# A hybrid attention and SSD layer on one core: output weights split early and loaded in the last attention pair, a four-step combine, and an output projection in a hand-written order

## The chip, the cores and the metric

One core of a Trainium2 chip. The metric is the device time of one execution in microseconds (us), as the median over runs. Engine names are those of the profile: PE (matrix multiplies), DVE, ACT and POOL (elementwise work), SP (issues most of the DMAs). POOL issues DMAs on a queue of its own.

## The reference

One decoder layer on x of shape (1, 2048, 1024), all in float32. An input projection gives q, k, v, the two gates z and the input of the SSD mixer. Attention runs three times per head (16 heads of 64) with dilations 1, 4 and 16 and a window of 128 steps; the three results are weighted by a softmax over their log-sum-exps. The SSD mixer is a chunked scan over 16 chunks of 128. Both branches are gated and normalised and meet in the output projection:

```python
y_att = (wts[0][..., None] * o1 + wts[1][..., None] * o2 + wts[2][..., None] * o3)
y_att = rms_norm(y_att.reshape(Bsz, S, D_ATT) * jax.nn.silu(z_att), att_norm_g[layer])
...
y_ssm = rms_norm(y.reshape(Bsz, S, D_SSM) * jax.nn.silu(z_ssm), ssm_norm_g[layer])
mix = jnp.concatenate([y_att, y_ssm], axis=-1)
out = jnp.einsum('bsd,de->bse', mix, w_out[layer])
x = layer_norm(alpha * x + out, ln_g[layer], ln_b[layer])
```

## The kernel before

Every large product is made of three matmuls on numbers split in two: a rounded high part (hi) and the remainder (lo), as hi·hi + hi·lo + lo·hi.

**Stages.** Projections of v, the gates and the convolution inputs come first, one `proj` per 128 output columns, 96 matmuls of 128x512 each. Then the eight projections of the SSD gate (`proj(32 + i)`, to about 685 us). From 685 to 1268 us q, k and the remaining gates are projected, with the 32 SSD units `ssd(n, g)` (chunk n, half g of the heads) between them; a unit stores its gated result y in `d_us`. Attention follows from 1268 us, in 8 pairs of heads, and then the output projection, to 2213 us.

**A pair of heads.** The loop `todo` runs over pairs, three dilations d, four blocks qd and two halves: 24 steps a pair. A step makes scores (L503), exponentials on ACT (L519), two steps later transposes (L532, copied to PT by DVE, L534) and one step after that the values (L552). After the last step of d=1 and of d=2 `statistics` transposes the minima and sums and SP stores them in `d_st` in short runs; `gather` reads them back as `cm` (L586). In the next pair DVE and ACT make the softmax weights from cm (`weights`, L593 to L603), SP stores them in `d_wd` and loads them broadcast over 64 partitions into `wb` (L616), and POOL combines the three results of the pair before (`combine`: L618, L627), gates them (L632), and SP stores the result in `d_ua`. Only pair 7 is combined by DVE, into four PT tiles. POOL also permutes q for d=1 (L467) and d=2 (L471) and issues the loads of k and q of the next pair (`load_qk`, L437), 1 MB each.

**The order.** Inside `tc.manual_schedule` PE, DVE, ACT and POOL take their instructions in the order in which the code is written; SP's order there, and all orders elsewhere, are set by the scheduler. An engine's queue is in order: an instruction that waits holds up all that stand behind it. Tiles of one name share a ring of buffers (three `v`, six `num`, three `wb`, four `qp`, three `P`), so a load waits until the tile that it replaces has been read.

**The output projection**, outside the manual order, multiplies 16 rows of 128 tokens by 2048x1024 weights: 32 products `product(n, br)` (row n; br=1 the SSD half, 0 the attention half) of 48 matmuls (L716 to L718). Weights are loaded raw, multiplied by the norm's gain and split on ACT, DVE or POOL (`prep_w`, L650 to L655) just ahead of use. `load_u` loads a row, splits it (L684, L685), sums its squares (L686, L688), and PE multiplies the sums by a column of ones (L690). `norm` is the layer norm.

## Time and profile before

| | |
|---|---|
| median of 3 runs | 2223.53 us (2221.91 to 2236.11) |
| profiled execution: its own time | 2223.12 us |
| profiled execution: span | 2221.3 us, mean granted PE clock 0.977 |
| instructions | 36859 |
| PE busy | 2152.9 us (97% of the span) |
| DVE, ACT, POOL busy | 1130.6, 867.1, 756.7 us |
| DMA | 321.69 MB, mean 145 GB/s |
| PE idle before L552 (values), ended by a PT copy of DVE | 27.7 us, 8 times |
| PE idle before L716 (product), ended by ACT's split of a weight (qp) | 12.2 us, once |

A row of the busy times reads: microseconds, share of the span, number of instructions. A row of a stretch gives its bounds and length, then busy time and instructions of PE, of PE's weight loads, of DVE, ACT and POOL, then the granted PE clock (1 is full), the share of the 16 DMA engines and GB/s. A row of the waits gives the waiting instruction, what ended the wait, the microseconds in all, the number of times and the longest. A row of the chain of waits or of the timeline begins with start and duration.

### The profile page before, as it was taken

The numbers are of one execution on the slowest core, as the hardware profiler recorded it, in microseconds if no ns is written. First come the engines' busy times: TensorE is split into PE (matmuls) and PEld (weight loads), VectorE is DVE, ScalarE is ACT, GpSimd is POOL, SyncE is SP. The second block draws the span as 40 slices with busy tenths as digits, with TensorE's granted clock in tenths as the row PEclk, the third lists the DMA queues.
The fourth block names the chain that finished last, engine by engine and source line by source line (L and its number), as shares of the span: only waits on it lengthen the run. The fifth ranks groups of instructions, "written<-read, shape, count | busy, mean of one in ns | idle before, by whom it ended". The sixth has DMA issues, their size and how long they took to land.

```text
span 2221.3 us, 36859 instructions
## 1 busy us (share of the span) xinstructions
PE 2152.9 (97%) x13968; PEld 1794.0 (81%) x13968; DVE 1130.6 (51%) x2931; ACT 867.1 (39%) x2318; POOL 756.7 (34%) x511
## 2 busy tenths in 40 slices
PE   8999999999999999999999999999989987999998
PEld 8999888888888888888888788778777865888886
DVE  4000265643003555454544278778777886655553
ACT  4101122223112233322355378778777864322221
POOL 3101010101112465555555313466544682221211
PEclk9999999999999999999999989999999987999999
DMA  8544222223125455555543536767677556422220
GB/s 284 176 134 135 82 68 76 67 76 91 58 85 178 174 190 174 177 182 175 189 140 126 199 122 189 225 186 201 185 209 213 153 168 184 135 97 95 82 83 29
DMA packets 239361, 321.69 MB, mean 145 GB/s; under 512 B 36304, under 2 KB 173648, under 8 KB 230992
## 3 DMA queue, kind: packets, MB, share of 16 engines
q1 hardware_dynamic: 234576, 285.78, 42.4%
q0 software_dynamic: 4608, 33.56, 4.0%
q8 instruction: 110, 1.80, 0.3%
q14 instruction: 67, 0.55, 0.1%
HBM read 205.65 MB, written 113.64 MB: 144 GB/s over the span
## 4 chain that ended last, share of the span: by engine, by line
PE 86%; DMA 7%; issue 2%; DVE 2%; POOL 1%; ACT 1%; SPq 1%; DVEq 0%; ACTq 0%; POOLq 0%
PE pp L111 14%; PE pp L109 14%; PE pp L110 14%; PE S L503 6%; PE N L552 6%; PE T L532 5%; PE S L716 4%; PE S L717 4%; PE S L718 3%; PE pp L153 2%; PE pp L154 2%; PE pp L152 2%; DMA d_st<-sT 2%; PE T L716 2%; PE T L717 2%
## 5 line engine op out<-in xcount | busy, mean ns | idle before, releaser
L109 PE MATMUL pp<-xh,whi 128*128 128x512 f32 x1408 | 550.2, 391 | 0.0
L110 PE MATMUL pp<-xl,whi 128*128 128x512 f32 x1408 | 549.5, 390 | 0.0
L111 PE MATMUL pp<-xh,wlo 128*128 128x512 f32 x1408 | 548.7, 390 | 0.0
L519 ACT ACTIVATE P<-P,st 128x256 f32<-128x256 f32 (+1 forms) x768 | 345.1, 451 | 94.5 <-DVE st L511 93.8
L111 PEld LDWEIGHTS pp<-xh,wlo 128*128 128x128 f32 x1408 | 264.3, 188 | 55.2
L109 PEld LDWEIGHTS pp<-xh,whi 128*128 128x128 f32 x1408 | 264.4, 188 | 54.7
L110 PEld LDWEIGHTS pp<-xl,whi 128*128 128x128 f32 x1408 | 264.4, 188 | 54.2
L511 DVE CUSTOM_DVE_ANT_0 P<-S,tb 128x256 f32<-128x256 f32 (+1 forms) x768 | 235.2, 362 | 105.7 <-PE S L503 51.2
L99 POOL TENSOR_TENSOR wlo<-wraw,whi 128x1024 fp32r<-128x1024 f32 x44 | 106.1, 2412 | 489.8 <-ACT whi L98 489.8
L552 PE MATMUL N<-PT,v 128*64 128x128 f32 x2400 | 183.3, 291 | 27.7 <-DVE PT L534 27.7
L534 DVE COPY PT<-T 128x512 f32<-128x512 f32 (+1 forms) x304 | 196.7, 677 | 3.6 <-PE T L532 3.6
L532 PE MATMUL T<-ident,P 128*128 128x128 f32 x1200 | 181.0, 289 | 4.7 <-DVE PT L534 3.7
L552 PEld LDWEIGHTS N<-PT,v 128*64 128x64 f32 x2400 | 133.7, 142 | 63.2 <-DVE PT L534 30.1
L532 PEld LDWEIGHTS T<-ident,P 128*128 128x128 f32 x1200 | 132.3, 144 | 28.7 <-DVE PT L534 4.2
L618 POOL TENSOR_TENSOR wb<-num,wb 128x2048 f32<-128x2048 f32 x21 | 96.2, 4583 | 157.9 <-ACT P L519 111.2
L519 ACT ACTIVATION_READ_ACCUMULATOR P<-P,st 128x1 f32 x768 | 143.9, 187 | 0.0
L126 DVE SCALAR_TENSOR_TENSOR ev<-pp,ev 128x512 f32<-128x512 f32 x64 | 44.1, 689 | 195.4 <-ACT ev L125 194.4
L503 PE MATMUL S<-kh,qp 64*128 64x256 f32 (+1 forms) x1024 | 130.8, 314 | 0.0
L503 PEld LDWEIGHTS S<-kh,qp 64*128 64x128 f32 x1024 | 92.1, 195 | 23.5 <-issue 22.5
L361 DVE TENSOR_SCALAR mt<-csb,cs 128x128 f32<-128x128 f32 x256 | 71.9, 352 | 76.1 <-DMA csb<-d_cs 76.1
L152 PE MATMUL pp<-vh,xh 128*128 128x384 f32 (+1 forms) x304 | 95.1, 320 | 7.0 <-ACT xh L182 5.5
L98 ACT CAST whi<-wraw 128x1024 fp32r<-128x1024 f32 x44 | 46.0, 1046 | 137.5 <-PE pp L110 134.8
(295 smaller groups left out, 3734.5 us busy)
## 6 DMA issues: line engine op xcount, KB each, us to landing
v<-d_v SPq DMA_DIRECT2D x24, 1024.0 KB
wb<-d_wd SPq DMA_DIRECT2D x48, 512.0 KB
wraw<-w SPq DMA_DIRECT2D x44, 512.0 KB
csb<-d_cs SPq DMA_DIRECT2D x32, 512.0 KB
d_v<-vt SPq DMA_DIRECT2D x64, 192.0 KB
d_za<-ev SPq DMA_DIRECT2D x32, 256.0 KB
d_xs<-cvo SPq DMA_DIRECT2D x8, 1024.0 KB
d_zs<-ez SPq DMA_DIRECT2D x8, 1024.0 KB
```

The lines of the kernel that those rows point to most:

```text
L109: nc.tensor.matmul(ps, hi[:, k, :], h, start=(k == 0), stop=False)
L110: nc.tensor.matmul(ps, hi[:, k, :], l, start=False, stop=False)
L111: nc.tensor.matmul(ps, lo[:, k, :], h, start=False, stop=(k == 7))
L152: nc.tensor.matmul(ps, h, vw[k][0], start=(k == 0), stop=False)
L503: nc.tensor.matmul(ov(sp[h][:, 256 * b:256 * b + w]), A["q"][d][x][hr, blk], kv(A["k"][y][hr]), start=(m == 0), stop=(m == 2))
L511: nc.vector.tensor_tensor_reduce(P[:, h, b, 256 - w:256], sp[h][:, c0:c0 + w], tab[:, h, tab.shape[2] - w:], 1.0, 3.0e38, OP.add, OP.min, ...
L519: nc.scalar.activation(p, p, AF.Exp, bias=stat(A, 0, d, h, blk), scale=-1.0, accum_out=stat(A, 1, d, h, blk))
L532: nc.tensor.transpose(tp[:, h, b], P[:, h, b, 128 * which:128 * which + 128], ident)
L534: nc.vector.tensor_copy(pt[:, :, bl[0]:2], tp[:, :, bl[0]:2])
L552: nc.tensor.matmul(nm[64 * h:64 * h + 64, bq * 128:bq * 128 + 128], v[:, k, 64 * h:64 * h + 64], pts[which][:, h, b], start=(f or not whic ...
L716: nc.tensor.matmul(ps, uh[:, e, :], wh, start=(e == 0), stop=False)
L717: nc.tensor.matmul(ps, uh[:, e, :], wl, start=False, stop=False)
```

## The change

1. **Weights split early.** A new `split_w` loads each row block of the output weights in two halves during the eight SSD gate projections, splits it with the gain on ACT and DVE, and stores both parts in a scratch array `d_wo` (8 MB read, 16 MB written).
2. **Rows split early.** In the SSD units of chunks 0 to 3 y is also split, into buffers of the names xdeh and xdel, and stored in `d_uh`.
3. **Weights loaded by POOL in pair 7**: W 8 to 11 into kh, kl, qh, ql in place of the next pair's k and q, W 12 to 15 and the parts of the first three SSD rows later in the pair; W 0 to 2 after it, W 3 to 7 after pair 7's combine.
4. **Combine in four steps**, written at four places of the next pair.
5. **Loads moved in the code**: k and q of the next pair at one place; tables and v of d=2 in their own pair.
6. **The output projection in the manual order**: `load_u` is divided into fetches, `split` and `squares`; the multiplication by ones stands between the two halves of the product; the addition into the residual is a function `add`.

Core of the diff:

```diff
+            def split_w(e):
+                g = gc[:, e:e + 1]
+                for hf in range(2):
+                    s = slice(hf * 512, hf * 512 + 512)
+                    raw = wo.tile([128, 512], F32, name="woraw")
+                    nc.sync.dma_start(raw, wout[e * 128:(e + 1) * 128, s])
+                    t = wo.tile([128, 2, 512], F32R, name="wot")
+                    nc.scalar.activation(t[:, 0], raw, AF.Copy, scale=g)
+                    nc.vector.scalar_tensor_tensor(t[:, 1], raw, g, t[:, 0].bitcast(F32), op0=OP.mult,
+                                                   op1=OP.subtract)
+                    nc.sync.dma_start(d_wo[e][:, :, s], t.bitcast(F32))
             for i in range(8):
                 proj(32 + i, fin_zs(i))
+                split_w(2 * i)
+                split_w(2 * i + 1)
...
+            if n < 4:
+                yh, yl = [sd.tile([128, 512], F32R, name=f"xde{p}") for p in "hl"]
+                y1 = y.rearrange("p c l -> p (c l)")
+                nc.scalar.copy(yh, y1)
+                nc.vector.tensor_tensor(yl, y1, yh.bitcast(F32), op=OP.subtract)
+                for p, t in enumerate((yh, yl)):
+                    nc.sync.dma_start(d_uh[g][n][:, p], v4(t.bitcast(F32)))
...
+        def load_w(e, name):
+            t = big(name)
+            nc.gpsimd.dma_start(t, d_wo[e].rearrange("p a c -> p (a c)"))
+            W[e] = t[:, 0:D], t[:, D:2 * D]
...
+        def squares(n, br):
+            u = raw.pop((n, br))
+            nc.scalar.activation(u, u, AF.Square)
+            sr[n, br] = f2(io.tile([128, 2, 256], F32, name="tb1", bufs=1))[:, 0:128]
+            nc.vector.tensor_reduce(sr[n, br], u.rearrange("p c t -> p t c"), axis=mybir.AxisListType.X, op=OP.add)
...
+                pss.append(ps)
+                if hf == 0:
+                    pn = psN.tile([128, 512], F32, name="N")
+                    nc.tensor.matmul(pn[:, 0:1], sr.pop((n, br)), one, start=True, stop=True)
...
                     if pr < 7:
-                        if (d, qd, half) == (0, 1, 0):
+                        if (d, qd, half) == (0, 3, 0):
                             pairs[pr + 1] = load_pair(pr + 1)
-                        if (d, qd, half) == (0, 3, 0):
                             load_qk(pairs[pr + 1], "q", d_qh, d_ql, io)
-                        if (qd, half) == (3, 1):
+                        if (qd, half) == (3, 1) and d < 2:
                             load_dil(pairs[pr + 1], d)
+                    elif (d, qd, half) == (0, 3, 0):
+                        for e, name in ((8, "kh_0"), (9, "kl_0"), (10, "qh"), (11, "ql")):
+                            load_w(e, name)
...
+                    if pr and (d, qd, half) == (0, 3, 1):
+                        load_dil(pairs[pr], 2)
...
+                    step = ((0, 3, 0), (1, 0, 0), (1, 2, 0), (2, 2, 0))
+                    if pr and (d, qd, half) in step:
+                        combine(pairs[pr - 1], step.index((d, qd, half)))
...
+            for i, (n, br) in enumerate(order):
+                ps = product(n, br)
+                if i == 0:
+                    weights(A, 0)
+                    residual(1)
+                    weights(A, 1)
+                if i == 1:
+                    fetch_parts(3, 1)
+                    fetch_raw(3, 1)
+                    for d in range(3):
+                        combine(A, d)
...
+                if i + 1 < len(order):
+                    if i == 3:
+                        split(0, 0, slice(7, 8))
+                    else:
+                        split(*order[i + 1])
+                    squares(*order[i + 1])
...
+                add(n, br, *ps)
+                if br == 0:
+                    norm(n)
```

Three places of the resulting orders.

SP where pair 5 passes into pair 6 (tb are the tables, v the values, d_st the statistics, cm the gather, d_ua the gated rows of pair 4). Before:

```order
L576 DMA d_st_119<-sT 64x1x32 x4
L633 DMA d_ua<-wb 128x16x128
L445 DMA tb_16177<-tabs 128x2x256
L447 DMA v<-d_v_102 128x16x128
L580 DMA d_st_119<-sT 16x16x8 x4
L586 DMA cm<-d_st_119 128x6x32
```

With the change:

```order
L601 DMA d_st_122<-sT 64x1x32 x4
L470 DMA tb_16733<-tabs 128x2x256
L660 DMA d_ua<-wb 128x16x128
L472 DMA v<-d_v_100 128x16x128
L605 DMA d_st_122<-sT 16x16x8 x4
L611 DMA cm<-d_st_122 128x6x32
```

The store of d_ua stands one place nearer to v and the statistics. At the starts of pairs 2 and 4 it is the same; at those of pairs 3, 5 and 7 it stands behind cm.

POOL from the combine of pair 5 to the first loads in pair 7 with the change (L659 is the gating multiply, L492 and L496 the permutes):

```order
L653 TENSOR_TENSOR wb<-wb 128x2048
L492 CAST qp<-qh 128x4x4x32 x4
L492 CAST qp<-ql 128x4x4x32 x4
L659 TENSOR_TENSOR wb<-wb 128x16x16x8
L496 CAST qp<-qh 128x512 x4
L496 CAST qp<-ql 128x512 x4
L675 DMA kh<-d_wo 128x2048
L675 DMA kl<-d_wo 128x2048
L675 DMA qh<-d_wo 128x2048
L675 DMA ql<-d_wo 128x2048
L644 TENSOR_TENSOR wb<-num,wb 128x2048 x2
```

The gating multiply stood ahead of the first permute before. In the earlier pairs the four DMAs are those of k and q, ahead of the combine as before.

DVE at the first products with the change (L714 is the reduce of the squares, L755 the addition of a product, L644 to L649 the combine of pair 7):

```order
L714 TENSOR_REDUCE tb_18596<-P 128x128
L751 RECIPROCAL st<-st 128x1
L755 SCALAR_TENSOR_TENSOR kh<-S,st,kh 128x512 x2
L644 TENSOR_TENSOR wb<-num,wb 128x2048 x2
L653 TENSOR_TENSOR wb<-wb 128x2048
L644 TENSOR_TENSOR wb<-num,wb 128x2048
L649 TENSOR_TENSOR PT<-wb 128x16x4x8 x4
L714 TENSOR_REDUCE tb_18698<-P 128x128
```

The combine stands between the reduce for product (1,1), first row, and the one for product (2,1), last row.

183 lines of the change are left out of this document (84 added, 99 removed).

## The prediction

> **What bounds the kernel now.** I read the profile's page first, to see which engine sets the pace; then busy time by stretches, to see where that engine falls short; then its waits and the chain of waits there.
>
> ```profile
> PE 2152.9 (97%) x13968; PEld 1794.0 (81%) x13968; DVE 1130.6 (51%) x2931; ACT 867.1 (39%) x2318; POOL 756.7 (34%) x511
> 490.00:685.00 195.00, 195.00 (x863) 161.44 (x862) 24.02 (x36) 42.21 (x61) 22.57 (x10) 1.00 0.29 86
> 685.00:1268.00 583.00, 582.64 (x3152) 479.76 (x3150) 273.28 (x540) 196.39 (x284) 293.52 (x219) 1.00 0.50 171
> 1406.60:1474.80 68.20, 63.98 (x741) 52.27 (x740) 53.70 (x239) 51.41 (x208) 38.73 (x28) 0.95 0.71 199
> 1749.20:1809.50 60.30, 56.28 (x631) 45.20 (x633) 53.12 (x211) 49.79 (x190) 35.69 (x12) 0.97 0.56 136
> 1809.50:1865.20 55.70, 32.73 (x155) 23.83 (x155) 34.16 (x32) 17.73 (x21) 25.20 (x8) 0.73 0.66 193
> 1865.20:2213.40 348.20, 348.20 (x1520) 282.08 (x1518) 189.51 (x267) 93.43 (x141) 74.43 (x31) 0.99 0.28 94
> ```
>
> PE is busy 97% of the span. In the z projections and the SSD stage (rows two and three) it never pauses, so work added there on other engines costs nothing unless it makes PE wait. PE loses time in two places. One is each attention pair: of 68.2 us, 4.2 are idle. The other is the passage from the last pair to the steady output projection, 1749.2 to 1865.2: 4.0 and 23.0 us idle, at a clock of 0.97 and 0.73. From 1865.2 on it is full again. PE's waits name the causes:
>
> ```profile
> PE N L552 <- DVE PT L534: 27.7, 8, 5.8
> PE S L716 <- ACT qp L650: 12.2, 1, 12.2
> DVE mm L593 <- DMA cm<-d_st: 28.2, 5, 6.6
> ```
>
> The first is five stalls of 4 to 6 us, one in each of pairs 2 to 6, and some short ones. DVE stands at L593 until cm has landed, and the PT copies that PE needs are behind it. The second is the wait for an output weight, split on ACT and DVE only then.
>
> **The passage, which the change empties.** After 1749.2 PE has pair 7 and the 32 products to do, until 2213.4: 464.2 us.
>
> ```profile
> 1749.20:1865.20 116.00, 12.41 (x28) 6.64 (x29) 0.85 0.61 163
> 1865.20:2213.40 348.20, 194.00 (x484) 91.57 (x484) 0.99 0.28 94
> 1422.20:1426.40 4.20, 0.00 (x1) 0.00 (x0) 2.12 (x13) 1.44 (x8) 0.00 (x0) 0.88 0.43 121
> 1426.40:1432.20 5.80, 5.77 (x42) 4.56 (x44) 5.09 (x23) 4.57 (x19) 0.00 (x0) 0.50 0.54 137
> 1861.30:1869.10 7.80, 6.61 (x15) 4.73 (x16) 6.35 (x5) 3.58 (x4) 4.99 (x2) 0.50 0.30 80
> ```
>
> The first two rows count line L716, a third of the products' matmuls: 484 of 512 lie in the steady stretch, so all 32 products take 348.2 x 512/484 = 368.3 us, one 11.5. A stalled pair loses 4.2 us of idling and then runs 5.8 us at half clock, which loses 2.9: 7.1 together, and an undisturbed pair takes 68.2 - 7.1 = 61.1. So 464.2 - 368.3 - 61.1 = **34.8 us** are lost in the passage. With weights that come split from DRAM, raw rows fetched ahead and the first three ssm rows stored split, product (0,1) needs nothing at its start that is made late: POOL issues its parts after five combine operations of pair 6. I take all 34.8 as saved and charge what replaces them.
>
> **A stall at the start of pair 7.** What happens in the other pairs:
>
> ```profile
> 1407.20 2.30 POOL L471 CAST qp<-ql 128x512 fp32r<-128x512 f32 x4
> 1409.44 0.59 POOL L437 DMA_DIRECT2D kh<-d_kh  x1
> 1415.98 0.53 POOL L437 DMA_DIRECT2D qh<-d_qh  x1 [5.41 <-PE T L532]
> 1409.71 8.50 DMA d_st<-sT
> 1418.35 5.85 DMA cm<-d_st
> 1831.81 2.17 DMA cm<-d_st
> 1424.22 0.19 DVE L593 TENSOR_TENSOR mm<-cm 128x32 f32<-128x32 f32 x1 [5.00 <-DMA cm<-d_st]
> ```
>
> The 4 MB of k and q leave POOL's queue as soon as its permutes end, just as SP stores the statistics and reads them back. The gather of cm takes 5.85 us there and 2.17 in pair 7, where no such load runs. In the new order POOL still issues k and q after both permutes, so the five stalls stay, whatever "loads spread" suggests: cost 0. In pair 7 W 8 to 11, again 4 MB, take that place: **+7.1**. Bounds: 0, if q's half (after the d=0 scores) misses cm, and 5.8 + 2.9 = 8.7 by the longest stall.
>
> The Trainium skill, "TensorE: Matmul & The Clock Gate", Part 1 (the HAM clock gate), says that the array runs at half clock after an idle window of about 3.4 us and is full again after about 3.4 us of sustained work. This trace shows 5.8 and 7.8 us at 0.50 after the work resumes. By the page a stall would cost 1.7 us of slow clock, and the two new stalls 3.4 us less than I charge. The rows decide.
>
> **d_ua in front of the statistics.** POOL's gating multiply (L632, now L659) comes 4.6 us later, behind the d=1 permute. On SP the store of d_ua then stands, at the starts of pairs 2, 4 and 6, directly ahead of v, the statistics and cm; before, it left at 1400.58.
>
> ```profile
> 1395.98 4.58 POOL L632 TENSOR_TENSOR wb<-wb 128x2048 f32<-128x2048 f32 x1
> 1400.58 0.37 SPq L633 DMA_DIRECT2D d_ua<-wb  x1
> 1400.60:1406.00 5.40, 5.40 (x76) 4.58 (x72) 3.93 (x21) 3.53 (x16) 5.40 (x10) 1.00 0.83 229
> 1411.00:1417.00 6.00, 6.00 (x78) 4.76 (x76) 4.79 (x28) 5.79 (x27) 1.02 (x2) 1.00 1.09 374
> ```
>
> Its 1.05 MB at the 374 GB/s of the loaded stretch take 2.8 us, at 229 GB/s 4.6. The DMA engines are full, so cm comes that much later: 3 x 2.8 = **+8.4**, bounds 0 and 13.8. In pairs 3, 5 and 7 the store stands behind cm and costs nothing.
>
> **A wait in the third product.** The hand order puts DVE's combine of pair 7 ahead of the reduce for product (2,1). PE multiplies that sum by `one` between the product's halves, and PE is in order. The chain, as it runs now:
>
> ```profile
> 1826.92 0.05 ACT num L562
> 1834.05 1.28 ACT L596
> 1843.78 13.79 DMA wb<-d_wd
> 1857.65 2.30 DVE wb L618
> 1863.32 1.21 DVE qp L651
> 1841.00:1857.00 16.00, 7.41 (x24) 5.52 (x24) 7.68 (x4) 1.67 (x2) 4.76 (x2) 0.74 0.97 207
> L688 DVE TENSOR_REDUCE tb<-P 128x128 f32<-128x1024 f32 x30 | 59.9, 1998 | 24.0 <-ACT P L686 23.4 <-PE N L690 0.6
> ```
>
> From the last values (1826.9) to the end of the combine (1863.3) it takes 36.4 us. The reduce adds 2.0. The table load of 1.28 falls away, since the order on ACT has the exponential ahead of the first square root. The wb loads keep the DMA engines 97% busy, and the new loads of W 0 to 2 (3.1 MB, 8.4 us at 374 GB/s) come at the same time: I add half, 4.2. That is 41.3 us after the values. PE gets there after a transpose (0.4) and two and a half products (28.8): 29.2. It waits 12.1 us and then runs 7.8 us at half clock, 3.9 more: **+16.0**. Behind the waiting matmul stand the other half of (2,1) and all later products. Without W 0 to 2 in the way it is 7.9 + 2.9 = 10.8; with all of them, and zt five us late behind d_ua on SP, 25. A product start that is some us late is covered by this wait.
>
> W 3 to 7 wait for the combine and are needed one and a half products later, 17 us, against 5.2 MB or 14 us: cost 0 by that cover, 5 without it.
>
> **SSD stage and z projections.** In eight SSD units the next unit's xdeh and xdel wait until the new stores have landed. The closest neighbours, as they run now:
>
> ```profile
> 787.46 2.21 POOL L383 TENSOR_TENSOR y<-y,zt 128x512 f32<-128x512 f32 x1
> 790.63 1.28 POOL L353 TENSOR_TENSOR xdel<-xde,xdeh 128x512 fp32r<-128x512 f32 x1
> 795.22 0.40 PE L388 MATMUL ss<-xdel,bsh 128*128 128x512 f32 x1
> 1240.38 2.43 DMA d_us<-y
> ...
> L352 ACT CAST xdeh<-xde 128x512 fp32r<-128x512 f32 x17 | 10.6, 621 | 36.4 <-POOL xde L350 36.4
> L382 DVE TENSOR_TENSOR y<-ss,xd 128x512 f32<-128x512 f32 x17 | 11.7, 688 | 7.0 <-POOL xd L381 5.7 <-PE ss L368 1.4
> ```
>
> y ends at 789.7. A cast (0.6) and a subtraction (0.7) of the new code, a store like that of d_us (2.4) and the next unit's xdel (1.3) end at 794.7, half a microsecond before PE needs it: **+1** for all, bounds 0 and 4. The splitting adds 64 short operations and 25 MB in some 180 us, 140 GB/s on top of the row's 86, where other rows reach 374: 0, bounds 0 and 3.
>
> **Sum.** -34.8 + 7.1 + 8.4 + 16.0 + 1.0 = -2.3. The profiled execution took 2223.12 us (span 2221.3; 0.4 below the median of 2223.53): **2220.8 us**. With the lower prices for d_ua, the wait and SSD it is 2206, with the upper ones and 3 for the z projections 2241. What is gained before the output projection is paid back in it and in pairs 2 to 7.
>
> **Rivals.**
> - The third product does not wait. If wb no longer takes 16.9 us for 3.1 MB but 8.4, as at 374 GB/s, the chain ends before PE arrives. 2220.8 - 16.0 = 2204.8, and 2196.4 if d_ua costs nothing either. For it: SP has less in front of these loads. Against it: wb moves at 207 GB/s at 97% share, with nothing beside it.
> - The loads do move. If k and q left POOL before the statistics, the five old stalls (35.5), the new one and d_ua's cost would go: 2220.8 - 35.5 - 7.1 - 8.4 = 2169.8. For it: pair 1, where k leaves as follows, has no stall.
>
> ```profile
> 1338.79 0.53 POOL L437 DMA_DIRECT2D kh<-d_kh  x1
> ```
>
>   Against it: in the new order k and q still stand behind both permutes.
> - Slower: the splitting starves the projections. SP alternates loads and stores of half rows, each store waiting for DVE, and the next projections' weights stand among them, some six halves to a projection of 22.4 us. Two projections of lead (45 us) over 32 halves allow 22.4/6 + 1.4 = 5.1 us a half. At 7 us, 5.4 projections last 42 instead of 22.4: 106 - 45 = 61 us late, 2282. For it: one in-order queue. Against it: a half costs about a load (2.4, as the store of the same size above), 0.6 and 0.7, 3.7 us, and two are in flight.
>
> **How the numbers follow.** Forecast 0.60, no wait 0.25, loads move 0.06, slower 0.09. A change of 1%, 22 us, is about what can be told from none. Below 2201.3 lie the moved loads, 0.15 of the no-wait case and 0.02 of the forecast: faster 0.23. Above 2245.8 lie the starved projections and 0.02 of the forecast: slower 0.11; within 1%: 0.66. The range 2194 to 2240 leaves out the moved loads, the slower case and the edges of the others.
>
> **What would show it.** Right: no idle PE from the last values to the first half of (2,1), then one wait of 8 to 20 us there on the reduce; a stall of 4 to 6 us in pair 7; stalls in pairs 2, 4 and 6 some 3 us longer than in 3 and 5. Wrong: PE waiting at the start of (0,1), PE idle in the z projections, cm in pair 7 landing in 2 us, or pairs of 61 us.

## The result, and the profile after

The changed kernel takes 2240.09 us in the median (20 runs, 2225.58 to 2245.73), the kernel before 2220.47 us on the same chips (20 runs, 2207.91 to 2242.68): a ratio of 1.0085, with a 95% interval of 1.0062 to 1.0108. It is slower by nearly 1%. The profiled execution of the changed kernel has a span of 2243.9 us against 2221.3 before; it is one of the longer runs, and the two traces differ by 22.6 us where the medians differ by 19.6.

The page's first rows say that PE does the same 13968 matmuls in about the same time (2145.6 us after, 2152.9 before); what has grown is the time in which it stands still. The DMA bytes grew from 321.69 to 363.66 MB.

```profile
PE 2145.6 (96%) x13968; PEld 1789.4 (80%) x13968; DVE 1155.1 (51%) x2940; ACT 866.7 (39%) x2321; POOL 759.6 (34%) x527
DMA packets 257219, 363.66 MB, mean 162 GB/s; under 512 B 37776, under 2 KB 175120, under 8 KB 246800
```

PE's waits, beside those in the prediction: the wait for PT copies has grown from 27.7 to 41.8 us, the wait for a split weight (12.2) is gone, and two waits for the reduce of the squares have come, 33.1 us together. The last row is new in the z projections.

```profile
PE N L577 <- DVE PT L559: 41.8, 7, 9.0
PE N L743 <- DVE tb L714: 33.1, 2, 17.6
...
PE pp L111 <- ACT ez L310: 4.8, 4, 1.7
```

The stretches show the places: the z projections, one of the pairs, the first products and the steady output projection (columns as before: PE, PE's weight loads, DVE, ACT, POOL, clock, DMA share, GB/s). In the z projections PE is idle 4.75 us of 200. From 1829 to 1905, the first products, it is idle 35.4 us of 76 at a clock of 0.78, with the DMA engines 92% busy; from 1905 on it is full.

```profile
490.00:690.00 200.00, 195.25 (x857) 159.91 (x856) 47.92 (x68) 62.01 (x91) 22.55 (x10) 1.00 0.67 209
...
1420.00:1490.00 70.00, 60.97 (x720) 49.96 (x716) 51.97 (x230) 49.35 (x200) 38.39 (x26) 0.93 0.64 183
...
1829.00:1905.00 76.00, 40.56 (x158) 31.57 (x155) 34.81 (x30) 11.72 (x16) 18.23 (x13) 0.78 0.92 290
1905.00:2234.90 329.90, 329.89 (x1451) 267.84 (x1449) 187.90 (x234) 78.75 (x112) 84.37 (x30) 1.00 0.25 85
```

To compare step by step I take PE's transposes of the statistics as marks: L570 before, L595 after, two in each pair, one behind the last values of d=1 and one behind the last values of the pair. In what follows a pair's **first part** runs from the mark that ends the pair before to its own first mark; the **passage** runs from the mark behind pair 7's last values (1826.81 before, 1829.22 after) to the end of PE's last matmul (2213.4, 2234.9).

| from the traces, us | before | after | difference | predicted |
|---|---|---|---|---|
| start of the span to the first transposes of attention | 1269.8 | 1275.3 | +5.5 | +1.0 |
| from there to the end of pair 6 | 479.3 | 488.4 | +9.2 | +8.4 |
| first part of pair 7 | 38.9 | 45.2 | +6.3 | +7.1 |
| rest of pair 7, and the passage | 425.5 | 426.0 | +0.5 | -18.8 |
| after PE's last matmul | 7.9 | 9.0 | +1.1 | 0 |
| sum | 2221.3 | 2243.9 | +22.6 | -2.3 |

Within the fourth row the rest of pair 7 shrank from 38.9 to 20.3 us, 18.5 of the 34.8 that were to be saved; the passage was to go from 386.6 to 386.6 - (34.8 - 18.5) + 16.0 = 386.3, and without any wait to 370.3. It went to 405.7. This is the miss: 19.4 of the 24.9 us between forecast and trace.

PE's row of instructions in the passage has two long waits, not one. The second stands where it was predicted, in product (2,1). The first stands in product (0,1), of which the prediction said that it needs nothing late at its start (L743 is the multiplication of the sums by `one`, in brackets the idle time and what ended it):

```profile
1853.53 0.58 PE L743 MATMUL N<-one,tb 128*128 128x1 f32 x2 [15.56 <-DVE tb L714]
1897.17 0.58 PE L743 MATMUL N<-one,tb 128*128 128x1 f32 x2 [17.56 <-DVE tb L714]
```

The start of (0,1) was not quite free either: PE waited there 1.3 and 1.0 us for the parts of the row.

The chain of waits leads back from the second wait through the first. POOL's gating multiply of pair 6 (L659), the store of d_ua (L660) and the load of zt (L839) come first. zt lands 18.46 us after its issue. DVE's multiplication by it (L841) stands ahead of the reduce (L714) that PE waits for, and the weights of pair 7 (L618, L619) stand behind both; then follow d_wd, the broadcast loads of wb (the last 15.37 us) and the combine, behind which stands the other reduce:

```profile
1825.80 4.55 POOL wb L659
1830.36 0.37 SPq L660
...
1830.78 18.46 DMA wb<-d_za
...
1849.36 0.09 DVE num L841
...
1851.57 1.91 DVE tb L714
1853.47 2.63 DVE mm L618
...
1862.70 9.25 DMA d_wd<-cm
...
1875.05 15.37 DMA wb<-d_wd
...
1895.34 1.79 DVE tb L714
```

What ran beside zt is told by the DMA view of 1821 to 1850: both queues together move 10.43 MB at 360 GB/s, and in 38 of its 40 slices the DMA engines are at least 80% busy. The prediction had counted 3.1 MB of W 0 to 2, which POOL issues only from 1860.5 on.

```profile
DMA packets 6606, 10.43 MB, mean 360 GB/s; under 512 B 1437, under 2 KB 3485, under 8 KB 6299
...
num<-d_uh POOLq DMA_DIRECT2D x6, 512.0 KB, 16.0
P<-d_us SPq DMA_DIRECT2D x6, 256.0 KB
v<-d_wo POOLq DMA_DIRECT2D x1, 1024.0 KB, 5.7
kl<-xc SPq DMA_DIRECT2D x2, 512.0 KB
kh<-xc SPq DMA_DIRECT2D x2, 512.0 KB
d_ua<-wb SPq DMA_DIRECT2D x1, 1024.0 KB
wb<-d_za SPq DMA_DIRECT2D x1, 1024.0 KB
```

### The profile page after: what moved, and what is told of

It reads as the page before. It is cut to its first block, busy times and chain, and to the rows that moved or that the text cites. A ratio compares the mean times of both kernels' runs of the same rounds, so it can differ in the third digit from the quotient of the medians.

```text
span 2243.9 us, 37059 instructions
## 1 busy us (share of the span) xinstructions
PE 2145.6 (96%) x13968; PEld 1789.4 (80%) x13968; DVE 1155.1 (51%) x2940; ACT 866.7 (39%) x2321; POOL 759.6 (34%) x527
## 2 busy tenths in 40 slices
DMA packets 257219, 363.66 MB, mean 162 GB/s; under 512 B 37776, under 2 KB 175120, under 8 KB 246800
## 4 chain that ended last, share of the span: by engine, by line
PE 80%; DMA 11%; DVE 3%; SPq 2%; issue 2%; ACT 2%; POOL 1%; ACTq 0%; DVEq 0%; POOLq 0%
PE pp L113 12%; PE pp L111 12%; PE pp L112 12%; PE S L528 6%; PE N L577 6%; PE T L557 6%; PE S L737 3%; PE S L739 3%; PE S L738 3%; DMA woraw<-wout 3%; DMA d_st<-sT 3%; PE pp L155 2%; PE pp L156 2%; PE pp L154 2%; PE T L737 2%
## 5 line engine op out<-in xcount | busy, mean ns | idle before, releaser
L577 PE MATMUL N<-PT,v 128*64 128x128 f32 x2400 | 179.4, 287 | 41.8 <-DVE PT L559 41.8
L644 POOL TENSOR_TENSOR wb<-num,wb 128x2048 f32<-128x2048 f32 x21 | 96.2, 4580 | 171.3 <-DMA wb<-d_wd 101.2
L714 DVE TENSOR_REDUCE tb<-P 128x128 f32<-128x1024 f32 x32 | 63.9, 1998 | 66.3 <-PE N L743 48.9
```

What stands on the lines that cost most here:

```text
L577: nc.tensor.matmul(nm[64 * h:64 * h + 64, bq * 128:bq * 128 + 128], v[:, k, 64 * h:64 * h + 64], pts[which][:, h, b], start=(f or not whic ...
```

## Experiments on the stalls of the pairs

Unless said otherwise each kernel is the changed one with one more edit. Of kernels with a single run I compare stretches of the trace, not times of 0.3%. The eight kernels of the next section and z_bufs leave the pairs as they are; there the first parts of pairs 2 to 6 sum to 230 to 237 us (236.6 in the changed kernel, 226.8 before), and the stalls of a pair vary by some 3 us from one execution to the next.

**u_early: the gating multiply ahead of the d=1 permute again.**

```diff
-                    step = ((0, 3, 0), (1, 0, 0), (1, 2, 0), (2, 2, 0))
+                    step = ((0, 3, 0), (1, 0, 0), (1, 2, 0))
                     if pr and (d, qd, half) in step:
                         combine(pairs[pr - 1], step.index((d, qd, half)))
+                        if (d, qd, half) == step[2]:
+                            combine(pairs[pr - 1], 3)
```

> The changed kernel, with POOL's gating multiply of the combine moved back ahead of the d=1 permute. Theory (the d_ua store stands in front of v, the statistics and cm in pairs 2, 4 and 6): the stalls of those pairs fall from 9.0, 8.2 and 8.4 us to the 5 to 6 us of pairs 3 and 5, the time from the end of one pair to the d=1 statistics of the next falls from 48.4 to 49.1 us to about 45.3, and the whole is 9 to 10 us shorter. Rival (those pairs are slower because the scheduler loads a later pair's v there): the three stalls stay above 8 us and the time stays within 2 us.

Measured: 2237.95 us (one run). The first parts of pairs 2 to 6 are 44.7, 45.3, 45.4, 45.4, 45.3, in sum 226.1: back to the 226.8 of before. That sum lies below all ten traces with the changed kernel's pairs (230 to 237), so the place of the gating multiply is what cost them this. The last values end at 1818.0 instead of 1829.2. Part of the gain is lost again: the first part of pair 7 takes 47.3 us instead of 45.2 and the passage 409.1 instead of 405.7, and the time of this one run is only 2 us below the changed kernel's median.

**k_early: the loads of k (and of W 8 and 9) ahead of the d=2 permute.**

```diff
                     if (d, qd, half) == (0, 0, 0):
+                        if pr < 7:
+                            pairs[pr + 1] = {"pr": pr + 1, "num": [], "tab": {}, "v": {}, "q": {0: []}, "k": []}
+                            load_qk(pairs[pr + 1], "k", d_kh, d_kl, qk[(pr + 1) % 2])
+                        else:
+                            load_w(8, "kh_0")
+                            load_w(9, "kl_0")
                         permute(pairs[pr], 2)
...
```

> The changed kernel, with the k loads of the next pair (in pair 7 W 8 and 9) written ahead of POOL's d=2 permute, so that they leave POOL's queue about 4.6 us earlier. Theory (the statistics and cm are starved by 8 KB packets of POOL's loads that start at the same moment): the stalls of pairs 2 to 7 (9.0, 5.2, 8.2, 5.6, 8.4, 5.0 us) fall under 2 us each, each pair's first part comes near the 38.9 us of the pair without a stall, and the whole is 35 to 48 us shorter, 2190 to 2205 us. Rival (the DMA engines are simply full at a pair's start, whatever the order): each stall shrinks by less than 2 us, the whole by less than 12.

Measured: 2253.09 us, ratio to the kernel before 1.0141 (1.0085 to 1.0197); first parts of pairs 2 to 6 50.8, 48.9, 48.3, 48.9, 48.9. Slower than both statements allowed for. In pair 3, whose stall is 8.0 us, k leaves POOL at 1481.51, now 3 us ahead of v, and in the eight microseconds from 1481 POOL's queue (q0) moves 2.08 MB and SP's (q1) only 0.10:

```profile
q0 software_dynamic: 282, 2.08, 72.6%
q1 hardware_dynamic: 204, 0.10, 4.5%
```

The store of the statistics behind v is then held 5.50 us in issue, and cm is issued at 1503.70 and landed at 1505.9. Earlier is worse.

**k_late: k, q and W 8 to 11 behind the first multiply of the combine on POOL, on top of u_early.** POOL waits there for wb, which is made from cm, so none of these loads can get ahead of cm.

```diff
+                    step = ((0, 3, 0), (1, 0, 0), (1, 2, 0))
+                    if pr and (d, qd, half) in step:
+                        combine(pairs[pr - 1], step.index((d, qd, half)))
...
                     if pr < 7:
                         if (d, qd, half) == (0, 3, 0):
                             pairs[pr + 1] = load_pair(pr + 1)
                             load_qk(pairs[pr + 1], "q", d_qh, d_ql, io)
```

> The changed kernel with the gating multiply ahead of the d=1 permute and, new here, the loads of k and q (in pair 7 of W 8 to 11) behind the first multiply of the combine on POOL, so that they really leave some 30 us later, when cm has long landed. Theory (the gather of cm is starved by whatever bulk load shares the DMA engines with it, so that only loads well away from it help): the stalls of pairs 2 to 7 fall to under 1 us, each first part to 38.9 us as in pair 1, the end of the values from 1818 to about 1780, and the whole is 35 to 45 us under the 2236 us of the run with the gating multiply alone, 2190 to 2200. Rival (the statistics are slow by themselves: 1024 packets of 32 bytes behind 1 MB of v on one queue): the stalls keep at least 3 us each and the gain stays under 15 us.

Measured: 2204.34 us, ratio 0.9917 (0.9891 to 0.9943). All first parts of pairs 1 to 7 are 38.8 to 39.2 us, and POOL shows the order that was meant:

```profile
1502.10 4.56 POOL L644 TENSOR_TENSOR wb<-num,wb 128x2048 f32<-128x2048 f32 x1 [22.39 <-DMA wb<-d_wd]
1506.60 0.60 POOL L462 DMA_DIRECT2D kh<-d_kh  x1
```

A pair runs without idling (a stretch of 62 us in pair 2: PE 61.64 at full clock). The last values end at 1781.0, 48 us earlier. The time misses the theory's 2190 to 2200 because the passage takes 415.1: the parts now come late there, with a wait of 18.3 us for them.

**b_late: the same move in the kernel before.** Its combine gets the loads behind its first multiply.

```diff
                 eng.tensor_tensor(wb, nums[d], wb, op=OP.mult)
+                if k and d == 0:
+                    load_kq(k)
...
```

> The kernel before, with one edit: k and q of the next pair leave POOL behind the first multiply of the combine, hence after the gather of cm, instead of right behind the permutes. Theory (the five stalls of 4 to 6 us in pairs 2 to 6 come from these 4 MB ahead of the statistics' short transfers, and this has nothing to do with the rest of the change): the time from the end of a pair's values to the next pair's d=1 statistics falls from 45.2 to 45.8 to about 39 us in pairs 2 to 6, some 33 us in all; with up to 6 given back elsewhere, 2188 to 2194 us, ratio 0.985 to 0.988. Rival (the old kernel gives it back, since q then comes too late for the permute of the next pair or the broadcast loads of wb run into the 4 MB): stalls of several us at the starts of pairs or in d=1, ratio 0.995 to 1.0.

Measured: 2210.14 us, ratio 0.994 (0.9913 to 0.9968). The stalls go as the theory says: pairs 2 to 6 are 38.85 us each, 32.5 us less in all. But the first part of pair 7 grows from 38.9 to 58.7. ACT has the split of an output weight (L656) ahead of pair 7's exponentials, and its raw weight, which SP issues right behind d_ua, has not landed:

```profile
1720.03 1.15 ACT L656 ACTIVATE kh<-kl,gc 128x1024 fp32r<-128x1024 f32 x1 [10.66 <-DMA kl<-wout]
```

PE waits 8.3 us there. Then, though busy without a break, it stays at half clock for 25 us more:

```profile
1725.00:1750.00 25.00, 25.00 (x170) 19.57 (x172) 12.73 (x68) 13.88 (x63) 0.00 (x0) 0.51 0.07 9
```

So the stalls are older than the change and can be removed without it. The ratio lies between the two ranges: the old kernel gives back 20 of the 32.5 us, at the start of pair 7 and for another reason than the rival's.

## Experiments on the passage

| kernel | edit | PE's waits of over 2 us in the passage | passage, us |
|---|---|---|---|
| changed | | 15.6 in (0,1), 17.6 in (2,1) | 405.7 |
| red_first | DVE's order | 4.5, 8.7, 16.7 | 401.4 |
| q_pool | POOL issues zt and d_ua | 14.4, 18.4 | 405.0 |
| zt_num | zt early in a num buffer | 2.7, 8.6 in (0,1), 22.0 in (2,1) | 405.0 |
| zt_red | both, residual rows on POOL | 19.4 in (1,1) | 389.2 |
| pass_fix | zt_num, red_first, ACT's order | 4.5, 3.4, 12.6 in (3,1) | 391.6 |
| no_w02 | pass_fix without loading W 0 to 2 | 2.1, 16.5 in (3,1) | 388.6 |
| spread | pass_fix, combine divided | 3.8, 7.5, 3.7 | 388.2 |
| both | spread without loading W 0 to 2 | 3.6, 3.9, 2.9 | 381.8 |

**red_first: only DVE's order.** The multiplication by zt stands behind the first reduce, and the reduce of the third row ahead of pair 7's combine.

```diff
-            for d in range(3):
-                (nc.vector if d == 2 else nc.gpsimd).tensor_tensor(A["num"][d], A["num"][d], zt, op=OP.mult)
+            for d in range(2):
+                nc.gpsimd.tensor_tensor(A["num"][d], A["num"][d], zt, op=OP.mult)
...
+                    squares(2, 1)
+                    nc.vector.tensor_tensor(A["num"][2], A["num"][2], zt, op=OP.mult)
                     for d in range(3):
                         combine(A, d)
...
```

> The changed kernel, with DVE's order alone altered: the multiplication by zt stands behind the reduce of product (0,1), and the reduce of product (2,1) stands ahead of pair 7's combine. Theory A (the two long waits of PE, 15.6 and 17.6 us, come from DVE's order): both fall under 5 us and most of 33 us is gained. Theory B (the chain of zt, statistics, cm, wb and combine is itself too long, and W 3 to 7 wait for the buffers that it frees): both waits fall, but product (0,0) then waits for W 3 to 7 until about 76 us after the last values as now; the last matmul comes only 0 to 12 us earlier.

Measured: 2240.45 us (one run), passage 401.4. The first wait falls to 4.5 us, but 8.7 us come in (1,1) and 16.7 in (3,1): a reduce that is moved ahead leaves the next one waiting. The 4.3 us gained are in theory B's range, but by other waits than those it names.

**q_pool: POOL issues pair 7's zt and pair 6's d_ua, so that SP's queue is free for the statistics.**

```diff
...
-            nc.sync.dma_start(f2(zt), d_za[7])
+            nc.gpsimd.dma_start(f2(zt), d_za[7])
+            nc.gpsimd.dma_start(*pairs[6]["ua"])
```

> The changed kernel, with pair 7's zt and the store of pair 6's d_ua issued by POOL in place of SP. Theory (SP's queue is held up behind the 1 MB of d_ua and zt, whose issue takes 11.2 us, so that the last statistics leave at 1843.8 where the values end at 1829.5): the statistics leave within 2 us of the values, cm lands by 10 us after them in place of 24, and the end of the combine comes 8 to 15 us earlier, as does the last matmul. Rival (the 16 DMA engines, 92% busy in that stretch, are the limit and not SP's queue): zt still lands some 18 us after its issue and the last matmul moves by less than 3 us.

Measured: 2241.36 us (one run), passage 405.0. zt leaves at 1826.69 and lands about 17 us later, nearly as before. The statistics now leave SP 3.6 us behind the last values instead of 14.6, and still cm is issued 21.4 us behind them, against 22.1. So SP's queue is not the limit.

**zt_num: zt comes on POOL's queue into a num buffer, ahead of the wait; the parts of the third row come behind the first product instead.**

```diff
-                        for n in range(3):
+                        for n in range(2):
                             fetch_parts(n, 1)
+                        zt7 = big("num", F32)
+                        nc.gpsimd.dma_start(zt7, d_za[7])
...
```

> The changed kernel, with pair 7's zt loaded by POOL into a num buffer ahead of the last values, and the parts of the third SSD row fetched after the first product in its place. Theory (10.4 MB stand in the DMA queues between 1821 and 1850 us, and zt, the statistics and cm come behind them): zt is there when the values end, the first wait of 15.6 us falls under 6, and with 1 MB less in the queue the combine ends 8 to 14 us earlier; the passage after the last values falls from 405.7 to 392 to 398 us. Rival (the combine chain after cm sets the end whatever zt does): the first wait moves into the second and the passage stays above 402 us.

Measured: 2240.64 us (one run), passage 405.0, the rival's number. zt leaves POOL at 1820.91, 4.4 us ahead of the last values, but lands 19.10 us later; the multiplication by it still stands ahead of the reduce, so that the wait in (0,1) is 8.6 us and the one in (2,1) grows to 22.0. (The 2.7 us are a wait for the parts at the start.)

```profile
1840.14 2.29 DVE L841 TENSOR_TENSOR num<-num 128x2048 f32<-128x2048 f32 x1 [15.77 <-DMA num<-d_za]
```

**zt_red: zt_num and red_first, and the first four residual rows on POOL's queue.**

```diff
-            nc.sync.dma_start(o, xc[n * 128:(n + 1) * 128, :])
+            (nc.gpsimd if n < 4 else nc.sync).dma_start(o, xc[n * 128:(n + 1) * 128, :])
```

> As the run with zt in a num buffer, and besides: zt's multiplication on DVE behind the reduces of products (0,1) and (2,1), the latter ahead of pair 7's combine, and the four residual loads (2 MB) moved from SP to POOL's queue behind W 0 to 2. Theory (both long waits come from bulk loads ahead of what the reduces and the combine need): PE waits under 5 us at each of the first products, the last matmul comes 376 to 386 us after the last values. Rival (the chain statistics, cm, d_wd, wb, combine, W 3 to 7 takes about 55 us after the values even with free queues, against the 46 us of four products): a wait of 8 us or more stays at the fourth product or at (0,0) and the passage is 386 to 395 us.

Measured: 2230.57 us (one run), passage 389.2, 16.4 less, in the rival's range. One long wait of 19.4 us is left, in (1,1), and that one is of this kernel's own making: ACT waits 26.6 us for a residual row, which now stands behind W 0 to 2 on POOL's queue, and pair 7's exponential (L621) and the squares of (1,1) stand behind it.

```profile
1859.58 1.06 ACT L719 ACTIVATE kh<-kh 128x1024 f32<-128x1024 f32 x1 [26.60 <-DMA kh<-xc]
```

**pass_fix: zt_num and red_first, the squares of (1,1) ahead of the weights of pair 7, the residual rows' activations behind them; the residual loads stay on SP.**

```diff
             squares(0, 1)
-            residual(0)
...
+                    fetch_parts(2, 1)
+                    squares(1, 1)
                     weights(A, 0)
-                    residual(1)
                     weights(A, 1)
+                    residual(0)
+                    residual(1)
...
```

> The changed kernel with the passage alone rearranged; stalls of the pairs and all loads of output weights stay as they are. zt comes by POOL into a num buffer, the multiplication with it stands behind the reduce of the first row on DVE, the squares of the second row stand ahead of the weights of pair 7, the third row's reduce ahead of its combine, and the activations of the residual rows behind the weights. Theory (the passage loses its time because instructions that PE needs stand on DVE and ACT behind others that wait for a load, one after the other; with all of them moved no wait is left that a product needs, though the same bytes move): both long waits go, the passage shrinks from 405.7 to 372 to 380 us, the time is 2210 to 2220 us, ratio 0.994 to 1.0. Rival (the DMA engines are full there, and a wait that is moved off one product comes back in a later one): the passage stays at 388 us or more as in the run with four residual rows on POOL's queue, 2226 us or more.

Measured: 2226.69 us, ratio 1.0005 (0.9977 to 1.0033); passage 391.6, the rival's numbers. The order on DVE and ACT together with zt's earlier load is worth 14.1 us, not the 26 to 34 of the theory: 12.6 us are left in (3,1), whose reduce stands behind the combine.

**no_w02: pass_fix with W 8 to 10 in the place of W 0 to 2, whose loads are left out.** The kernel leaves out the right weights of three of the attention half's eight blocks; it is there for its time alone.

```diff
-            for e, name in ((0, "qp"), (1, "qp"), (2, "v")):
-                load_w(e, name)
+            for e in range(3):
+                W[e] = W[8 + e]
```

> The kernel with the passage rearranged, without the three loads of W 0 to 2 (3.1 MB): the products of the attention half use W 8 to 10 in their place, so what is left out is the right weights for three of the eight blocks of that half; the number of matmuls is the same. Theory (with the order on DVE and ACT mended, what is left of the passage's waits is that the broadcast loads of wb share full DMA engines with W 0 to 2 and the parts of two rows): the wb loads land some 8 to 10 us earlier (3.1 MB at the 300 to 374 GB/s of that stretch), the wait of 12.6 us for the reduce behind the combine falls to 5 us or less, the passage to 378 to 384 us. Rival (the broadcast loads are slow by themselves, 207 GB/s with nothing beside them in the kernel before, and the chain through cm and d_wd is what is late): the wait stays at 9 us or more and the passage at 388 us or more.

Measured: 2223.07 us (one run), passage 388.6, wait 16.5: the rival's numbers. Counted from the last values (1826.14 in pass_fix, 1824.08 in no_w02), the first broadcast table is there 8.2 us earlier, which is what the theory said of the loads. The wait behind the combine grows all the same, since PE, less delayed before, reaches it 7.2 us earlier, and the third table gains 3.3 us only. DVE's combine in pass_fix and then in no_w02:

```profile
1873.58 2.29 DVE L644 TENSOR_TENSOR wb<-num,wb 128x2048 f32<-128x2048 f32 x1 [15.79 <-DMA wb<-d_wd]
...
1883.21 2.29 DVE L644 TENSOR_TENSOR wb<-num,wb 128x2048 f32<-128x2048 f32 x1 [0.19 <-DMA wb<-d_wd]
```

```profile
1863.34 2.29 DVE L644 TENSOR_TENSOR wb<-num,wb 128x2048 f32<-128x2048 f32 x1 [5.19 <-DMA wb<-d_wd]
...
1877.81 2.29 DVE L644 TENSOR_TENSOR wb<-num,wb 128x2048 f32<-128x2048 f32 x1 [3.13 <-DMA wb<-d_wd]
```

**spread: pass_fix, with pair 7's combine divided: its first multiply in the second product, the rest behind the reduce of (3,1) in the third.**

```diff
-                    for d in range(3):
-                        combine(A, d)
+                    combine(A, 0)
...
+                if i == 2:
+                    squares(3, 1)
+                    combine(A, 1)
+                    combine(A, 2)
...
```

> The kernel with the passage rearranged, and one thing more: the first multiply of pair 7's combine on DVE stands in the second product as before, the other two and the addition stand behind the reduce of the fourth row, in the third product; the loads of W 4 to 7 follow them. All bytes stay. Theory (the last wait of 12.6 us, and 16.5 with the competing bytes taken away, comes from the place of the fourth row's reduce behind the three broadcast loads of wb, which land 7 us after one another): that wait falls to 3 us or less, the passage from 391.6 to 374 to 382 us, the time is 2209 to 2219 us. Rival (DMA engines are full, so W 3 to 7 and the first attention row come late instead): waits of 8 us or more for a weight or for the row in products five and six, passage at 387 us or more.

Measured: 2226.2 us (one run), passage 388.2, in the rival's range. The wait behind the combine is gone (0.4 us), and waits for loads take its place:

```profile
PE T L737 <- DMA num<-d_uh: 7.5, 1, 7.5
PE S L737 <- DMA num<-d_uh: 3.8, 1, 3.8
PE S L739 <- DVE num L708: 3.7, 1, 3.7
```

**both: spread without the loads of W 0 to 2**, as in no_w02.

> The kernel with the divided combine, without the three loads of W 0 to 2 (3.1 MB; the attention half uses W 8 to 10 in their place, with the same number of matmuls). Each of the two steps alone moved the passage by some 3 us only. Theory (order and bytes each hold one wait: with the reduce out of the way PE waits for parts and weights, with the bytes away it waits for the reduce; only both together free it): the waits after the first product sum to 5 us or less, the passage is 372 to 380 us, the time 2208 to 2214 us on the clock of the run with the divided combine. Rival (the chain of cm, d_wd and broadcast loads is late by itself, whatever the order and the bytes): waits of 8 us or more, passage at 384 us or more.

Measured: 2219.64 us (one run), above the theory's 2208 to 2214; passage 381.8, between the two ranges and near the theory's. Alone the two steps give 2.9 and 3.4 us, together 9.8: one hides behind the other. Of 35.4 us that the changed kernel loses in the passage against the 370.3 without waits, the order on DVE and ACT with zt's earlier load carries 14.1, the place of the last reduce and the bytes of W 0 to 2 together 9.8. 11.5 stay, with four short waits (10.8 us) of which three are for loads.

## The projections, and a better version

**z_bufs: four raw buffers instead of two for the output weights' halves.**

```diff
-                    raw = wo.tile([128, 512], F32, name="woraw")
+                    raw = wo.tile([128, 512], F32, name="woraw", bufs=4)
```

> The changed kernel with four buffers instead of two for the raw halves of the output weights (woraw) in the gate projections, and nothing else. Theory (ACT stands before the next weight half until its load has landed, and the evacuation of the gate's psum waits behind it): the PE gaps of 4.7 us between 597 and 634 us shrink to 2 or less, and the first transposes of attention come 2 to 3 us earlier than 1275.33. Rival (SP's queue of alternating loads and stores is the limit, however many buffers): the gaps stay at 4 or more.

Measured: 2238.71 us (one run); two gaps of 4.25 us together instead of four of 4.75; the first transposes at 1274.2 lie within what kernels without this edit show (1273.8 to 1276.8). The size is the rival's, but its cause is not shown. In the changed kernel ACT stands before the next half until its load has landed, 72.5 us in 30 waits, and the evacuation of the gate's product, for which PE waits, stands behind it. With four raw buffers that wait all but goes (2.7 us, once), and at the same instruction ACT waits for the store of an earlier split half, whose ring `wot` still has two buffers. More buffers there were not tried. The changed kernel, then z_bufs:

```profile
ACT wot L326 <- DMA woraw<-wout: 72.5, 30, 5.8
...
ACT wot L326 <- DMA d_wo<-wot: 52.2, 23, 5.6
```

**best: k_late, zt_red and z_bufs together.**

> All of it together: gating multiply early, k and q loads (W 8 to 11) behind the first multiply of the combine, zt in a num buffer, reduces ahead, residuals on POOL's queue, and four buffers in place of two for the raw halves in the z projections. Theory (the losses are separate and add): 2243.9 less some 48 us in the pairs, 20 to 30 in the passage and 3 to 4 in the z projections: 2160 to 2175 us, under the kernel before by 2 to 3 per cent. Rival (the loads taken from the start of the pairs come back in pair 7, which then carries 11 MB between the combine's start and the products): the pairs gain, the passage is as long as in the changed kernel, 2190 to 2205 us.

Measured: 2195.74 us, ratio 0.9884 (0.9842 to 0.9925): the rival's range, and the losses do not add. Its passage takes 408.7, with a wait of 16.8 us for the parts and one of 18.7 behind the residual row on ACT.

**best2: in best, W 12 to 14 leave ahead of pair 6's last multiply, the parts and zt ahead of its gating multiply, and ACT's order is that of pass_fix.**

```diff
+                    if pr == 7 and (d, qd, half) == (1, 2, 0):
+                        for e, name in ((12, "v"), (13, "qp"), (14, "qp")):
+                            load_w(e, name)
...
+                    elif (d, qd, half) == (2, 0, 0):
+                        for n in range(2):
+                            fetch_parts(n, 1)
+                        zt7 = big("num", F32)
+                        nc.gpsimd.dma_start(zt7, d_za[7])
+                        combine(pairs[6], 3)
```

> The best version so far, with three more moves in the passage: W 12 to 15 leave POOL ahead of the last combine of pair 6, the parts of the first two rows and zt ahead of its gating multiply, and the squares of the second row and the weights of pair 7 stand ahead of the residual rows on ACT, whose activation waited 25.3 us for the load of a residual row. Theory (the 16.8 us wait is for parts that leave POOL late, the 18.7 us wait for an in-order ACT behind a load): the first wait falls to 0 to 8 us and the second to 0 to 5; the 408.7 us from the last values' transpose to the last PE instruction become 380 to 390, the time 2166 to 2177 us. Rival (the passage is bound by its bytes, and a wait only moves, as in the run with zt in a num buffer): the passage stays at 400 us or more, the time at 2187 or more.

Measured: 2180.96 us, ratio 0.9802 (0.9742 to 0.9862). The passage is 391.7, 17 us shorter: the wait of 16.8 becomes 3.0 and that of 18.7 in (1,1) goes, but waits of 6.5 and 2.4 in (2,1) and 6.1 in (3,1) come in their place, so the theory has the direction and too large a size. This is the version with the lowest time: the change with its loads behind cm and its passage rearranged, faster than the kernel before by 2.0% (1.4 to 2.6). Its stretch from the last values to the steady projection, still with full DMA engines:

```profile
1779.00:1847.00 68.00, 48.62 (x183) 37.87 (x183) 31.17 (x32) 11.87 (x17) 19.90 (x19) 0.86 1.02 312
```

**best3: best2 with the divided combine of spread.**

> The best version so far (u and the loads of k and q moved, passage rearranged) with the same division of pair 7's combine over two products. Theory: the wait of 6.1 us behind the combine goes, the passage shrinks from 391.7 to 380 to 388 us, the time is 2170 to 2178 us. Rival (the waits for the parts, 6.5 us and less, come from full DMA engines and only grow): passage at 390 us or more, 2178 to 2184 us.

Measured: 2188.59 us, ratio 0.9815 (0.9739 to 0.9891), passage 396.8. The theory falls: the reduce still waits 7.7 us. Full DMA engines, as the rival has it, fit this, but were not tried apart; the time lies above both ranges, and the ratio does not tell this version from best2.

## Why the prediction was wrong

**What bounds the kernel, and the saving: right.** The pairs and the passage are where PE loses time, before and after. The wait for a split weight is gone, and PE is full from 1905 on. The 34.8 us were there to be saved: the rest of pair 7 gave 18.5 of them at once.

**Stall at the start of pair 7: right**, +6.3 against +7.1. **d_ua ahead of the statistics: right in kind, and near in size partly by luck.** It is +9.2 in the seven pairs against +8.4, in pairs 2, 4 and 6 as predicted, and u_early takes the loss away. But over the ten traces with these pairs the first parts of pairs 2 to 6 grow by 7.0 us in the mean: 5.2 in pairs 2, 4 and 6, and 1.8 in pairs 3 and 5, where d_ua stands behind cm and was charged nothing. **"The five stalls stay": right**, and k_late and b_late show their cause: without loads ahead of cm they vanish. The stalls of pairs 2, 3 and 7 (those of 4 and 6 are 8.2 and 8.4 us, that of 5 is 5.6):

```profile
1436.64 1.12 PE L577 MATMUL N<-PT,v 128*64 128x128 f32 x8 [9.03 <-DVE PT L559]
1504.94 1.12 PE L577 MATMUL N<-PT,v 128*64 128x128 f32 x8 [5.23 <-DVE PT L559]
...
1784.51 1.12 PE L577 MATMUL N<-PT,v 128*64 128x128 f32 x8 [5.04 <-DVE PT L559]
```

**The step that failed is "A wait in the third product", +16.0, with the sentence on the passage that product (0,1) "needs nothing at its start that is made late".** The one wait in (2,1), taken as 12.1 us, was 17.6; the wait in (0,1), at nothing in the sum, was 15.6, with 2.3 more at its start. The passage lost 35.4 us against 370.3. (That PE's idle time there is 35.4 us too is chance: the slow clock behind the two waits adds some 5 us, and 370.3, which counts 11.5 us a product, is that much too high.) Two things were missed.

First, the middle of (0,1) was not looked at. The prediction asked what its start needs. Its middle needs a reduce on DVE, and in DVE's order the multiplication by zt stands ahead of that reduce. The trace has it 18.46 us on its way, and the wait was 15.6 us. The rule that the prediction applied to POOL and SP (name what is queued behind a waiting instruction) was not applied to DVE here.

Second, the bytes. Half of W 0 to 2, 4.2 us, was charged for competition. In the 29 us from 1821 the DMA engines moved 10.43 MB almost without a pause: d_ua, zt, six loads of P, four residual rows, the parts of three rows and W 15. In the sum none of them stands; zt behind d_ua appears in an upper bound, at five us. zt took 18.46 us, and 17 to 19 in q_pool and zt_num, from another queue and another place; d_wd took 9.25 (3.59 before), cm left SP at 1851.35, and the chain from the last values to the reduce behind the combine, taken as 41.3 us, took 67.9 (1829.2 to 1897.1). zt_num, no_w02 and spread show that no single edit mends it: a wait that is moved off one product comes back in a later one. That the bytes set the length of zt's load is inferred from its neighbours; only the 3.1 MB of W 0 to 2 were taken away in a run.

A third piece, smaller: the two 128x32 operations at the head of that chain took 2.62 and 4.50 us instead of 0.19, beside POOL's multiplications by zt.

**z projections, charged at 0 with a bound of 3: wrong**, 4.75 us of idle PE. The rival had the next projections' weights come late; PE waited instead for ACT, which stood before its next half. What SP's in-order queue adds to that was not tried apart. With the SSD units, where hardly anything is seen (PE idle 0.5 us of 585, 0.4 of 583 before), the two together are +5.5 against +1. Attention starts at 1273.8 to 1276.8 in twelve traces of kernels that are equal up to there, and at 1269.8 and 1268.0 in two with the old code, so this loss is real, and its size uncertain by some 3 us. **The end**, +1.1, was not in the sum at all.

Two of the prediction's own signs of being wrong came: PE waiting at the start of (0,1), and PE idle in the z projections. Its sum with all upper prices, 2241 us, is near the time by chance, since it holds no wait in the middle of (0,1).

**The slow clock was charged too high for this trace.** The prediction took 5.8 and 7.8 us at half clock after a stall from rows of before. After, it is 3.6 us after the stall in pair 2 and 3.8 after the wait in (2,1):

```profile
1436.70:1440.10 3.40, 3.40 (x24) 2.73 (x24) 3.26 (x15) 2.15 (x9) 0.00 (x0) 0.50 0.22 46
...
1897.10:1901.00 3.90, 3.83 (x10) 3.15 (x11) 3.86 (x6) 0.26 (x1) 0.00 (x0) 0.50 1.04 399
```

These two agree with the 3.4 us that the Trainium skill, "TensorE: Matmul & The Clock Gate", Part 1, states and that the prediction set aside. But after the wait in (0,1) it is 6.5 us, and after PE's waits of over 3.4 us in all the traces it is mostly 3.3 to 6.6, with a median of 4.6, so one price does not fit all.

## What to carry to other kernels

When work is moved out of a busy passage, list by bytes everything that is still to be loaded or stored there, not only the loads that the change adds: here 10.43 MB ahead of W 0 to 2. For an in-order engine that the next matmul waits for, write down what stands ahead of the needed instruction in the middle of a product as well as at its start, and what each of those waits for. Large loads that may leave at any time belong behind the short transfers that the next step needs: tied to an instruction that depends on the gather, they cost the pairs nothing, and k_late, with the gating multiply moved as well, takes 36 us less than the changed kernel.

## What the runs showed of the hardware

**DVE and POOL exclude each other for some operations.** POOL's multiplication took 6.67 us where it usually takes 4.58, while DVE multiplied two operands of its own beside its start (1849.36 to 1851.65). DVE's 128x32 operation with two operands then ended at 1856.1, the next at 1860.6, each as POOL's ended. The reduce between them, with one operand, ran at its usual 1.91.

```profile
1849.37 6.67 POOL L841 TENSOR_TENSOR num<-num,wb 128x2048 f32<-128x2048 f32 x1 [19.03 <-DMA wb<-d_za]
```

```profile
1853.47 2.62 DVE L618 TENSOR_TENSOR mm<-cm 128x32 f32<-128x32 f32 x1
1856.13 4.50 DVE L619 TENSOR_TENSOR mm<-mm,cm 128x32 f32<-128x32 f32 x1
```

In pass_fix, where POOL's multiplications are over by then, the same two take 0.19 us each. The Trainium skill, "SBUF — State Buffer", section "SBUF: two separate sides", says that such operations hold a pair of ports that both engines share, for their whole length; these rows agree.

**A busy PE can stay at half clock.** At the start of attention PE is busy for 27.14 of 27.2 us and the granted clock is 0.50 all the time; in b_late it happened again for 25 us.

```profile
1276.40:1303.60 27.20, 27.14 (x183) 21.23 (x183) 12.06 (x64) 16.30 (x76) 1.05 (x2) 0.50 0.71 243
1303.70:1326.00 22.30, 22.30 (x264) 18.32 (x265) 20.53 (x83) 18.26 (x69) 4.52 (x8) 1.00 0.21 61
```

The first part of pair 0 takes 50.2 to 51.7 us in every kernel here, that of pair 1 38.9. Why the clock does not return there was not tried.

**Issuing a load can hold the engine for 11 us.** SP's instruction that issues the load of zt took 11.22 us where such an issue mostly takes 0.4, and the statistics stood behind it. In zt_num other loads stand behind d_ua, and their two issues took 13.33 us. In both stretches the DMA engines are full (375 and 386 GB/s); that this is the reason was not tried apart.

```profile
1830.36 0.37 SPq L660 DMA_DIRECT2D d_ua<-wb  x1
1830.78 11.22 SPq L839 DMA_DIRECT2D wb<-d_za  x1
...
1843.82 2.03 SPq L605 DMA_DIRECT2D d_st<-sT  x4
```

```profile
1826.61 13.33 SPq L696 DMA_DIRECT2D P<-d_us  x2
```
